# Three products of split operands in a pooling mixer, and attention's weight splits on VectorE

## Chip, cores and metric

One core of one Trainium2 chip runs the whole kernel. The metric is the device time of one execution in microseconds (us), as the median of the runs shown.

## What is computed

A two-layer backbone on 512 latent and 256 context tokens of 1024 channels, in float32. Layer 0 mixes tokens by pooling, layer 1 by attention; each layer ends in a squared-ReLU MLP, and each sub-layer is modulated by a shift, a scale and a gate that come from a conditioning vector. Cut to the part that the change touches:

```python
sh1, sc1, g1, sh2, sc2, g2 = jnp.split(s_lat @ ada_w[i] + ada_b[i], 6, axis=-1)   # the same for the context
a = rms_norm(h, norm_g[i, 0]) * (1 + sc1) + sh1
# pool_mix: each of 4 channel groups has its window (2, 4, 8, 16) and its own 256x256 matrix w
s = (sum of a over the window) / count - a
y = jnp.einsum("blgc,gcd->blgd", s, w) * pool_scale
h = h + g1 * y
m = rms_norm(h, norm_g[i, 1]) * (1 + sc2) + sh2
h = h + g2 * (square(relu(m @ w1)) @ w2)
```

Layer 1 is grouped-query attention with 8 query and 4 key heads of 128 channels, then its own MLP and a last RMSNorm of the latent tokens.

## The kernel before

Activations lie with channels on the partitions: `h_lat` (8 tiles of 128x512) and `h_ctx` (8 tiles of 128x256). A product of two float32 operands is made in one of two ways. Most are split: each operand is a pair hi + lo of type F32R, and three products (hi·hi, hi·lo, lo·hi, the table `PASSES`) are summed in PSUM. `hilo` (L85 to L87) makes such a pair: ScalarE writes hi, then VectorE, or the engine handed in, writes lo = source - hi. `load_w` loads 128x1024 of weights into one of two `raw` buffers and splits it. The other way is a plain F32 matmul, which stands in the trace as two records per instruction.

**The scales, shifts and gates.** `ada_w` comes in 12 blocks per layer. `ada0_products(b)` multiplies a block's four tiles with the conditioning vectors (L187) and copies the result to a row (L190, ScalarE); `ada0_done(b, row)` turns the row by four transposes (L196), and VectorE reduces it (L199), adds the bias (L201) and makes of it the scales `am` (L155, blocks 2, 3, 8, 9) or the gate `gp` (L163, blocks 4 and 5). Blocks 6 and 7 are the MLP's shift, blocks 8 and 9 its scale.

**The mixer of layer 0** runs so: the tokens are turned and normalized into `turned`; `pool_tile(k)` makes channel tile k of the pooled tokens with six plain F32 matmuls against banded matrices (L621) into a `mm` place of PSUM (two places of 4 KB), and ScalarE (odd k, L625) or VectorE (even k, L627) copies it to `pooled`. All eight tiles come first. The scale (1 + sc1) is not on the tokens but on the matrix: `scaled_weights` writes one copy of `pw` for the latent tokens (L634, ScalarE) and one for the context (L635, VectorE). Then `mix(dt)` makes output tile dt with four plain F32 matmuls (L645), `mixed(dt)` adds it to h under the gate (L348, VectorE), and `squares` gathers the squares for the next norm: ScalarE squares (L266), VectorE adds (L267). Blocks 4, 3, 5 and 6 stand between the eight tiles dt. After the loop come block 8's products, the sums of the squares (L282), the reciprocal root on GpSimd (L286), block 7's products, the spreading of the roots (L297), and then the MLP's first product, whose operand is made tile by tile: L705 and L727 on VectorE, L716 on ScalarE (for the context L703, L713, L714, L725), and used by L732.

**Attention** has for each key head two weight loads for the next queries (`q_fill`) and two for the output matrix (`wos`). Before, both of a `q_fill` and the second of each `wos` have their lo written by GpSimd, ten in all. Around them VectorE carries the softmax: maximum (L941), its negative bias (L943), the exponential on ScalarE (L946), the reciprocal (L948), the scaling (L949); and for the next queries the mean square (ScalarE L867, VectorE L868) and the rotation (L879 to L883). L961 are the transposes of the probabilities, L974 the values, L986 the output matrix, L860 the projections.

**What sets the order.** Every engine works through its queue in order. In the mixer TensorE's queue is the order in which the code is written; VectorE's and ScalarE's are set by the scheduler up to the line `stats = ps_aux()`, and from there to the MLP's first product by the code as well. All loads are on SyncE's queue, in the order of the code; a load waits there until its buffer is free, and all behind it wait too. `block6` and `block8` land in the places of `turned`, so they wait for the last pooled tile.

Of the kernel before, what the change touches and what calls it, by code (L numbers as in the profile page):

```python
# [14 lines left out]
P = 128  # L15
# [32 lines left out]
def dit_block_kernel(ctx: ExitStack, tc: tile.TileContext, xT, cols, adab, adaw, w1, w2, wqkv, wo,  # L48
# [119 lines left out]
    def ada0_products(b):  # L168

        ps = ps_aux()  # L170
        for u in range(4):
            if (b, u) in ((5, 3), (9, 3)):

                t = new(raws, [P, 1024], F32, "raw")
                nc.sync.dma_start(t, adaw[0, b, u])
            elif b in landing:
                t = landing[b][:, u]
                nc.sync.dma_start(t, adaw[0, b, u])
            elif early:
                t = early.pop(0)  # L180
            else:
                t = new(*praw)
                nc.sync.dma_start(t, adaw[0, b, u])
# [75 lines left out]
    def squares(acc, k, w, c0, n, place=None):  # L259
# [4 lines left out]
        else:  # L264
            sq = new(sc, [P, w, n], F32, "sc")
            act.activation(sq, hs(k, k + w, c0, n), AF.Square)  # L266
            dve.tensor_tensor(acc, acc, sq, op=ALU.add)  # L267
# [340 lines left out]
    pooled = [new(ap_, [P, 2, 2, T], F32, "act").rearrange("p a b n -> p (a b) n") for _ in range(2)]  # L608

    def pool_tile(k):  # L610

        g, ps = k // 2, ps_mm()
        w = WINDOWS[g] // 2
        for s, c0, n in segs:
            for i in range(n // P):
# [4 lines left out]
                o = c0 + i * P - PAD  # L620
                pe.matmul(ps[:, o + a : o + b], turned[s][:, i, k * P : k * P + P], bands[:, g, e, a:b],  # L621
                          start=i == 0, stop=i == n // P - 1, skip_group_check=True)
        dst = pooled[k // 4][:, k % 4]
        if k % 2:
            act.activation(dst, ps[:, :T], AF.Copy)  # L625
        else:
            dve.tensor_copy(dst, ps[:, :T])  # L627

    aw = [new(wp, [P, KT, 256], F32, "w") for _ in range(2)]

    def scaled_weights(k0, k1):

        for k in range(k0, k1):
            act.activation(aw[0][:, k], pw[:, k], AF.Copy, scale=am[0][0][:, k, 0:1])  # L634
            dve.tensor_scalar(aw[1][:, k], pw[:, k], am[0][0][:, k, 1:2], None, op0=ALU.mult)  # L635
# [3 lines left out]
    def mix(dt):  # L639

        ps = ps_mm()
        for s, c0, n in segs:
            for kc in range(2):
                k = dt // 2 * 2 + kc
                pe.matmul(ps[:, c0 : c0 + n], aw[s][:, k, dt % 2 * P : dt % 2 * P + P], pooled[k // 4][:, k % 4, c0 : c0 + n],  # L645
                          start=kc == 0, stop=kc == 1)
        return ps
# [3 lines left out]
    def mixed(dt, ps):  # L651
        for s, c0, n in segs:
            add_gated(dt, ps[:, c0 : c0 + n], gp, c0, n)
            if dt < KT - 1:
                accs[s] = squares(accs[s], dt, 1, c0, n)
            else:
                tails.append(new(sc, [P, 1, n], F32, "sc"))
                act.activation(tails[s], hs(dt, dt + 1, c0, n), AF.Square)

    row = ada0_products(2)  # L660
    pool_tile(0)
    ada0_done(2, row)
    scaled_weights(0, 4)
    for k in range(1, 8):
        pool_tile(k)

    for b, tag in ((6, "m_hi"), (8, "m_lo")):
        landing[b] = big.tile([P, 4, D], F32, tag=tag, name=f"block{b}")
    for dt in range(8):
        if dt % 2 == 0:  # L670
            b = (4, 3, 5, 6)[dt // 2]
            row = ada0_products(b)
        if dt == KT - 1:
            ws = [load_w(w1[0, t]) for t in range(2)]
        ps = mix(dt)
        if dt % 2 == 0:
            ada0_done(b, row)
            if b == 3:
                scaled_weights(4, 8)
        mixed(dt, ps)  # L680
    row = ada0_products(8)
# [5 lines left out]
    rrs = [rstd_cols(n, [accs[s], tails[s]], stats[:, 4 * s : 4 * s + n // P]) for s, _, n in segs]  # L687
    ada0_done(8, row)
    row = ada0_products(7)
    rbs = [spread(rrs[s], n, ps_aux()[:, :n]) for s, _, n in segs]  # L690
# [44 lines left out]
    for u in range(len(units) + 2):  # L735
# [7 lines left out]
        if u == 1:  # L743
            last = ada0_products(9)
            ada0_done(7, row)
# [292 lines left out]
    for n in range(8 * NKV):  # L1038
        g, half, i = n // 8, n // 4 % 2, n % 4
        if i == 0 and half == 0 and g + 1 < NKV:  # L1040
            fill = q_fill(g + 1, [load_w(wqkv[8 + 2 * (g + 1) + u], pool) for u in range(2)])
# [10 lines left out]
        if half == 0 and i == 1:  # L1052
            wos = [load_w(wo[2 * g + j], (dve, pool)[j]) for j in range(2)]
# [126 lines left out]
```

## Time and profile before

| | |
|---|---|
| median of 3 runs | 1269.24 us (1268.84 to 1270.68) |
| profiled execution, its own time | 1270.8 us |
| span of its trace | 1268.8 us |
| TensorE matmul busy | 97% |
| VectorE busy | 81% |
| ScalarE busy | 46% |
| GpSimd busy | 12% |

The profile is of one execution. Matmul (PE) and weight load (PEld) overlap; the ends of matmuls are modelled. Names such as `mm<-act,w` say what an instruction writes and reads; L followed by a number is a line of the kernel before. In the chain of waits each piece starts where the one ahead of it ended, so its length is what that work took of the path. In the change the lines from L621 on stand 6 to 18 lower in the file; texts here use the lines of before.

### The profile page before, as it was taken

The numbers are of one execution on the slowest core, as the hardware profiler recorded it, in microseconds if no ns is written. First come the engines' busy times: TensorE is split into PE (matmuls) and PEld (weight loads), VectorE is DVE, ScalarE is ACT, GpSimd is POOL, SyncE is SP. The second block draws the span as 40 slices with busy tenths as digits, with TensorE's granted clock in tenths as the row PEclk, the third lists the DMA queues.
The fourth block names the chain that finished last, engine by engine and source line by source line (L and its number), as shares of the span: only waits on it lengthen the run. The fifth ranks groups of instructions, "written<-read, shape, count | busy, mean of one in ns | idle before, by whom it ended". The sixth has DMA issues, their size and how long they took to land.

```text
span 1268.8 us, 20479 instructions
## 1 busy us (share of the span) xinstructions
PE 1236.7 (97%) x8150; PEld 1103.4 (87%) x8150; DVE 1026.2 (81%) x1752; ACT 588.7 (46%) x1052; POOL 149.1 (12%) x128
## 2 busy tenths in 40 slices
PE   7999999999999999999999999999999999999997
PEld 6567888899999999999888899899988898989896
DVE  6564999788989888866888378888899989898976
ACT  6455523443444444433465254445555444445443
POOL 0000000122121322231012121211000000000002
PEclk8999999999999999999999999999999999999998
DMA  9676414333433333311122011211223232323111
GB/s 352 259 275 219 147 67 153 113 117 117 149 114 133 121 127 120 121 67 34 45 81 85 23 61 34 67 34 67 84 67 116 100 133 71 130 76 125 67 34 67
DMA packets 41311, 138.67 MB, mean 109 GB/s; under 512 B 4736, under 2 KB 8064, under 8 KB 41088
## 3 DMA queue, kind: packets, MB, share of 16 engines
q1 hardware_dynamic: 41216, 137.36, 30.7%
q8 instruction: 64, 1.05, 0.3%
q14 instruction: 31, 0.25, 0.1%
HBM read 135.25 MB, written 2.10 MB: 108 GB/s over the span
## 4 chain that ended last, share of the span: by engine, by line
PE 62%; issue 27%; DVE 7%; ACT 2%; POOL 1%; DMA 1%; SPq 0%; POOLq 0%; DVEq 0%; ACTq 0%
PE mm L490 10%; PE aux L490 10%; PE aux L860 6%; PE mm L371 6%; PE aux L459 5%; PE mm L439 5%; PE aux L439 4%; PE aux L986 3%; PE aux L187 2%; PE mm L645 2%; PE mm L732 1%; PE aux L974 1%; PE aux L961 1%; PE mm L938 1%; PE mm L621 1%
## 5 line engine op out<-in xcount | busy, mean ns | idle before, releaser
L490 PE MATMUL mm<-act,w 128*128 128x512 f32 (+1 forms) x1224 | 237.7, 346 | 1.8 <-DVE h_lat L348 1.8
L490 PE MATMUL aux<-act,w 128*128 128x512 f32 (+1 forms) x1224 | 239.0, 346 | 0.2
L490 PEld LDWEIGHTS mm<-act,w 128*128 128x128 f32 x1224 | 195.1, 189 | 32.7 <-DVE h_lat L348 2.0
L490 PEld LDWEIGHTS aux<-act,w 128*128 128x128 f32 x1224 | 195.0, 189 | 29.5 <-DVE h_lat L348 0.6
L86 ACT ACTIVATE w<-raw 128x1024 fp32r<-128x1024 f32 x106 | 110.2, 1055 | 79.2 <-PE aux L490 37.8
L87 DVE TENSOR_TENSOR w<-raw,w 128x1024 fp32r<-128x1024 f32 x96 | 117.3, 1225 | 28.2 <-ACT w L86 27.5
L348 DVE SCALAR_TENSOR_TENSOR h_lat<-aux,mod,h_lat 128x512 f32<-128x512 f32 (+1 forms) x204 | 126.5, 629 | 16.0 <-PE aux L490 14.4
L428 POOL TENSOR_TENSOR sc<-pair 128x512 f32<-128x512 f32 x55 | 76.7, 1402 | 319.2 <-DVE h_lat L348 104.9
L348 DVE SCALAR_TENSOR_TENSOR h_lat<-mm,mod,h_lat 128x512 f32<-128x512 f32 (+1 forms) x140 | 97.7, 700 | 6.1 <-PE mm L490 3.7
L371 PE MATMUL mm<-m_m_hi,w 128*128 128x512 f32 (+1 forms) x320 | 92.4, 351 | 0.1
L860 PE MATMUL aux<-w,a_m_hi 128*128 128x256 f32 (+1 forms) x384 | 86.3, 320 | 0.0
L219 DVE SCALAR_TENSOR_TENSOR mc<-raw,s_f,mc 128x512 f32<-128x512 f32 x112 | 83.4, 763 | 2.0 <-DMA raw<-in_dram 1.3
L439 PE MATMUL mm<-m_m_hi,mc 128*128 128x256 f32 x384 | 71.0, 283 | 0.0
L286 POOL TENSOR_TENSOR sm<-sm,neghalf 128x2 f32<-128x2 f32 (+1 forms) x11 | 8.9, 811 | 509.9 <-DVE sm L284 509.9
L860 PEld LDWEIGHTS aux<-w,a_m_hi 128*128 128x128 f32 x384 | 63.4, 190 | 5.0
L459 PE MATMUL aux<-m_c,w 128*128 128x256 f32 x528 | 65.2, 283 | 0.0
L371 PEld LDWEIGHTS mm<-m_m_hi,w 128*128 128x128 f32 x320 | 56.1, 189 | 10.0 <-ACT r L379 0.8
L459 PEld LDWEIGHTS aux<-m_c,w 128*128 128x128 f32 x528 | 64.2, 192 | 0.0
L860 PE MATMUL aux<-w,a_m_lo 128*128 128x256 f32 (+1 forms) x192 | 61.2, 319 | 0.0
L439 PEld LDWEIGHTS mm<-m_m_hi,mc 128*128 128x128 f32 x384 | 60.7, 192 | 0.5
L371 PE MATMUL mm<-m_m_lo,w 128*128 128x512 f32 (+1 forms) x160 | 56.0, 351 | 0.0
L439 PE MATMUL mm<-m_m_lo,mc 128*128 128x256 f32 x192 | 54.4, 283 | 0.0
(244 smaller groups left out, 2509.1 us busy)
## 6 DMA issues: line engine op xcount, KB each, us to landing
raw<-in_dram SPq DMA_DIRECT2D x157, 512.0 KB, 3.3
praw<-in_dram SPq DMA_DIRECT2D x34, 512.0 KB, 8.1
fin<-in_dram SPq DMA_DIRECT2D x24, 512.0 KB, 4.2
pair<-in_dram SPq DMA_DIRECT2D x22, 512.0 KB, 4.6
block<-in_dram SPq DMA_DIRECT2D x8, 512.0 KB, 6.2
h_lat<-in_dram SPq DMA_DIRECT2D x4, 512.0 KB, 6.0
w<-in_dram SPq DMA_DIRECT2D x4, 512.0 KB, 10.7
out_dram<-fin SPq DMA_DIRECT2D x8, 256.0 KB, 2.6
```

The costliest lines, as they stand in the source:

```text
L86: act.activation(hi, src, AF.Copy)
L87: lo_eng.tensor_tensor(lo, src, hi.bitcast(F32), op=ALU.subtract)
L187: pe.matmul(ps[o : o + P // CG, :512], s_w[:, kt], t[:, kk * 512 : kk * 512 + 512], start=kt < CG, stop=kt >= KT - CG)
L219: dve.scalar_tensor_tensor(acc[:, s], w, scal, acc[:, s], op0=ALU.mult, op1=ALU.add)
L348: dve.scalar_tensor_tensor(h, ps, gate[:, dt, s : s + 1], h, op0=ALU.mult, op1=ALU.add)
L371: pe.matmul(ps[:, c0 : c0 + cn], lhs, ms(m, ax, k, c0, cn), start=k + wx + ax == 0, stop=k == KT - 1 and wx == 1)
L428: eng.tensor_tensor(t, x, y, op=how)
L439: pe.matmul(places[n], w[:, wx, k * P : k * P + P], inputs[n][ax][:, k], start=k + wx + ax == 0, stop=k == 3 and wx == 1)
L459: pe.matmul(pc[:, t * 256 : t * 256 + 256], ws[k // 4][:, wx, k % 4 * P : k % 4 * P + P], ms(m, ax, k, SEQ, CTX), start=k + wx + ax == 0, ...
L490: pe.matmul(ps, lhs, a[:, t, ax, c0 : c0 + n], start=t + wx + ax == 0, stop=t == 1 and wx == 1)
L860: pe.matmul(ps, lhs, ws[u][:, wx, o : o + width], start=k + ax + wx == 0, stop=k == KT - 1 and ax == 1)
L986: pe.matmul(ps[:, :256], ws[j][:, wx, dt * P : dt * P + P], o[:, ax, j], start=j + wx + ax == 0, stop=j == 1 and ax == 1)
```

## The change

1. The mixer's products are split. `scaled` takes a pooled tile out of PSUM, under the scale (1 + sc1) of its tokens, as a pair: ScalarE writes hi (512 and 256 columns apart), VectorE lo, by one instruction with the PSUM tile as its input. `pw` is split once, unscaled. `mix` has twelve F32R matmuls where it had four F32 ones.
2. The pooled tiles no longer come all first: four ahead of the loop, the others within it after dt = 1 to 4. Odd tiles use two of the four `aux` places instead of a `mm` place.
3. Blocks 2 and 4 are turned ahead of the loop (4 between tiles 1 and 3), blocks 3, 5 and 7 in it, block 6 at its end, block 8 behind the sums of squares; block 7 no longer stands between the roots and the MLP. Block 6's and 8's loads come behind block 9's first three on SyncE's queue.
4. In the loop GpSimd adds the squares (twelve adds), not VectorE.
5. The ten lo splits of attention's weights that GpSimd had go to VectorE.

```diff
@@ -171,7 +171,7 @@
         for u in range(4):
             if (b, u) in ((5, 3), (9, 3)):
-                t = new(raws, [P, 1024], F32, "raw")
+                t = new(mc, [P, 1024], F32, "mc")
                 nc.sync.dma_start(t, adaw[0, b, u])
             elif b in landing:
                 t = landing[b][:, u]
@@ -256,7 +256,7 @@
         k0, k = (k.start // 4, slice(k.start % 4, (k.stop - 1) % 4 + 1)) if isinstance(k, slice) else (k // 4, k % 4)
         return m[1][x][k0][:, k, c0 - SEQ : c0 - SEQ + n]
-    def squares(acc, k, w, c0, n, place=None):
+    def squares(acc, k, w, c0, n, place=None, eng=dve):
         if acc is None:
             acc = new(accp[0], [P, w, n], F32, accp[1]) if place is None else place
@@ -264,7 +264,7 @@
         else:
             sq = new(sc, [P, w, n], F32, "sc")
             act.activation(sq, hs(k, k + w, c0, n), AF.Square)
-            dve.tensor_tensor(acc, acc, sq, op=ALU.add)
+            eng.tensor_tensor(acc, acc, sq, op=ALU.add)
         return acc
     def all_squares(c0, n, place=None, k1=KT):
@@ -605,11 +605,17 @@
                 act.activation(t, t, AF.Copy, scale=rr[:, i : i + 1])
             else:
                 dve.tensor_scalar(t, t, rr[:, i : i + 1], None, op0=ALU.mult)
-    pooled = [new(ap_, [P, 2, 2, T], F32, "act").rearrange("p a b n -> p (a b) n") for _ in range(2)]
+    pooled = {}
     def pool_tile(k):
-        g, ps = k // 2, ps_mm()
+        g = k // 2
+        if k % 2:
+            places = [ps_aux(), ps_aux()[:, :CTX]]
+        else:
+            ps = ps_mm()
+            places = [ps[:, :SEQ], ps[:, SEQ:T]]
         w = WINDOWS[g] // 2
         for s, c0, n in segs:
             for i in range(n // P):
@@ -617,33 +623,35 @@
                 a = PAD if e == 1 else PAD + 1 - w
                 b = PAD + P if e == 2 else PAD + P + w
-                o = c0 + i * P - PAD
-                pe.matmul(ps[:, o + a : o + b], turned[s][:, i, k * P : k * P + P], bands[:, g, e, a:b],
+                o = i * P - PAD
+                pe.matmul(places[s][:, o + a : o + b], turned[s][:, i, k * P : k * P + P], bands[:, g, e, a:b],
                           start=i == 0, stop=i == n // P - 1, skip_group_check=True)
-        dst = pooled[k // 4][:, k % 4]
-        if k % 2:
-            act.activation(dst, ps[:, :T], AF.Copy)
-        else:
-            dve.tensor_copy(dst, ps[:, :T])
-    aw = [new(wp, [P, KT, 256], F32, "w") for _ in range(2)]
-    def scaled_weights(k0, k1):
-        for k in range(k0, k1):
-            act.activation(aw[0][:, k], pw[:, k], AF.Copy, scale=am[0][0][:, k, 0:1])
-            dve.tensor_scalar(aw[1][:, k], pw[:, k], am[0][0][:, k, 1:2], None, op0=ALU.mult)
+        return k, places
+    def scaled(k, places):
+        if k % 2 == 0:
+            pooled[k // 2] = new(ap_, [P, 2, 2, T], F32R, "act")
+        for s, c0, n in segs:
+            hi, lo = (pooled[k // 2][:, k % 2, x, c0 : c0 + n] for x in range(2))
+            a = am[0][0][:, k, s : s + 1]
+            act.activation(hi, places[s], AF.Copy, scale=a)
+            dve.scalar_tensor_tensor(lo, places[s], a, hi.bitcast(F32), op0=ALU.mult, op1=ALU.subtract)
+    aw = [new(wp, [P, KT, 256], F32R, "w") for _ in range(2)]
+    for k in range(0, KT, 4):
+        hilo(aw[0][:, k : k + 4], aw[1][:, k : k + 4], pw[:, k : k + 4])
     accs = [None, None]
     def mix(dt):
         ps = ps_mm()
-        for s, c0, n in segs:
-            for kc in range(2):
-                k = dt // 2 * 2 + kc
-                pe.matmul(ps[:, c0 : c0 + n], aw[s][:, k, dt % 2 * P : dt % 2 * P + P], pooled[k // 4][:, k % 4, c0 : c0 + n],
-                          start=kc == 0, stop=kc == 1)
+        for n, (kc, (wx, ax)) in enumerate((kc, p) for kc in range(2) for p in PASSES):
+            lhs = aw[wx][:, dt // 2 * 2 + kc, dt % 2 * P : dt % 2 * P + P]
+            for s, c0, w in segs:
+                pe.matmul(ps[:, c0 : c0 + w], lhs, pooled[dt // 2][:, kc, ax, c0 : c0 + w], start=n == 0, stop=n == 5)
         return ps
     tails = []
@@ -652,42 +660,52 @@
         for s, c0, n in segs:
             add_gated(dt, ps[:, c0 : c0 + n], gp, c0, n)
             if dt < KT - 1:
-                accs[s] = squares(accs[s], dt, 1, c0, n)
+                accs[s] = squares(accs[s], dt, 1, c0, n, eng=pool)
             else:
                 tails.append(new(sc, [P, 1, n], F32, "sc"))
                 act.activation(tails[s], hs(dt, dt + 1, c0, n), AF.Square)
     row = ada0_products(2)
-    pool_tile(0)
+    tile0 = pool_tile(0)
     ada0_done(2, row)
-    scaled_weights(0, 4)
-    for k in range(1, 8):
-        pool_tile(k)
-    for b, tag in ((6, "m_hi"), (8, "m_lo")):
-        landing[b] = big.tile([P, 4, D], F32, tag=tag, name=f"block{b}")
+    scaled(*tile0)
+    scaled(*pool_tile(1))
+    row = ada0_products(4)
+    scaled(*pool_tile(2))
+    ada0_done(4, row)
+    scaled(*pool_tile(3))
     for dt in range(8):
-        if dt % 2 == 0:
-            b = (4, 3, 5, 6)[dt // 2]
-            row = ada0_products(b)
-        if dt == KT - 1:
+        ps = mix(dt)
+        if dt in (0, 3):
+            row = ada0_products(3 + 2 * (dt > 0))
+        elif dt == 4:
+            ada0_done(5, row)
+        mixed(dt, ps)
+        if dt == 1:
+            ada0_done(3, row)
+        if dt in (1, 2, 3, 4):
+            scaled(*pool_tile(dt + 3))
+        if dt == 4:
+            for b, tag in ((6, "m_hi"), (8, "m_lo")):
+                landing[b] = big.tile([P, 4, D], F32, tag=tag, name=f"block{b}")
             ws = [load_w(w1[0, t]) for t in range(2)]
-        ps = mix(dt)
-        if dt % 2 == 0:
-            ada0_done(b, row)
-            if b == 3:
-                scaled_weights(4, 8)
-        mixed(dt, ps)
-    row = ada0_products(8)
+        if dt == 5:
+            row = ada0_products(7)
+        elif dt == 6:
+            ada0_done(7, row)
+    row = ada0_products(6)
     by_hand.enter_context(tc.manual_schedule(engines={mybir.EngineType.DVE, mybir.EngineType.Activation}))
     stats = ps_aux()
     rrs = [rstd_cols(n, [accs[s], tails[s]], stats[:, 4 * s : 4 * s + n // P]) for s, _, n in segs]
+    ada0_done(6, row)
+    row = ada0_products(8)
+    rbs = [spread(rrs[s], n, ps_aux()[:, :n]) for s, _, n in segs]
     ada0_done(8, row)
-    row = ada0_products(7)
-    rbs = [spread(rrs[s], n, ps_aux()[:, :n]) for s, _, n in segs]
     m = new_m("m")
     units = [u for k in range(0, KT, 2) for u in ((0, k, 1), (0, k + 1, 1), (1, k, 2))]
@@ -742,7 +760,6 @@
         if u == 1:
             last = ada0_products(9)
-            ada0_done(7, row)
         elif u == 3:
             ada0_done(9, last)
     ws = [load_w(w1[0, 2 + t]) for t in range(2)]
@@ -1038,7 +1055,7 @@
     for n in range(8 * NKV):
         g, half, i = n // 8, n // 4 % 2, n % 4
         if i == 0 and half == 0 and g + 1 < NKV:
-            fill = q_fill(g + 1, [load_w(wqkv[8 + 2 * (g + 1) + u], pool) for u in range(2)])
+            fill = q_fill(g + 1, [load_w(wqkv[8 + 2 * (g + 1) + u]) for u in range(2)])
         if 0 < n < 8 * NKV - 1:
             scores((n + 1) // 8, (n + 1) // 4 % 2, (n + 1) % 4, st)
         if i < 2 or g == NKV - 1:
@@ -1050,7 +1067,7 @@
         if i == 1 and n > 1:
             run(*prev)
         if half == 0 and i == 1:
-            wos = [load_w(wo[2 * g + j], (dve, pool)[j]) for j in range(2)]
+            wos = [load_w(wo[2 * g + j]) for j in range(2)]
         if pend:
             pend.pop()()
         turn(i, st)
```

**Where the order of the work changes.** ScalarE's queue at the first pooled tiles. `aux_328` (now `aux_330`) is block 2's product and `aux_422` (now `aux_374`) block 4's, each copied to its row by L190; L625 copies pooled tiles, L634 scales the matrix; in the change L638 is the hi of a pooled tile, and L86 here the hi of `pw`. Before:

```order
L190 ACTIVATE sc_337<-aux_328 128x512
L625 ACTIVATE act_324<-mm_364 128x768
L634 ACTIVATE w_326<-pw,am_137 128x256 x4
L625 ACTIVATE act_324<-mm_380 128x768
L625 ACTIVATE act_325<-mm_396 128x768
L625 ACTIVATE act_325<-mm_412 128x768
L190 ACTIVATE sc_431<-aux_422 128x512
```

Now:

```order
L190 ACTIVATE sc_339<-aux_330 128x512
L638 ACTIVATE act_357<-mm_341,am_137 128x512
L638 ACTIVATE act_357<-aux_362,am_137 128x512
L638 ACTIVATE act_357<-aux_363,am_137 128x256
L638 ACTIVATE act_357<-mm_341,am_137 128x256
L86 ACTIVATE w_324<-pw 128x1024 x2
L190 ACTIVATE sc_383<-aux_374 128x512
```

The four hi of tiles 0 and 1, which need block 2's scales, and the two hi of `pw` stand ahead of block 4's row, whose transposes TensorE now has two pooled tiles earlier than the loop.

VectorE's queue in attention, where the second head's queries have been projected and the weights for the third are split. Before (both splits are on GpSimd):

```order
L948 RECIPROCAL ri_7611<-rs_7609 128x1
L949 TENSOR_SCALAR r_7608<-r_7608,ri_7611 128x768
L868 TENSOR_SCALAR sm_7870<-sm_7870 128x4
L879 TENSOR_TENSOR sc_7881<-aux_7614,tabs 128x512
L87 TENSOR_TENSOR mc_7663<-aux_7664,mc_7663 128x256
```

Now (L965, L966, L885 and L896 are the lines L948, L949, L868 and L879 of before):

```order
L965 RECIPROCAL ri_7693<-rs_7691 128x1
L966 TENSOR_SCALAR r_7690<-r_7690,ri_7693 128x768
L87 TENSOR_TENSOR w_7809<-raw_7810,w_7809 128x1024
L87 TENSOR_TENSOR w_7814<-raw_7815,w_7814 128x1024
L885 TENSOR_SCALAR sm_7952<-sm_7952 128x4
L896 TENSOR_TENSOR sc_7963<-aux_7696,tabs 128x512
L87 TENSOR_TENSOR mc_7745<-aux_7746,mc_7745 128x256
```

Two splits now stand between a probability's scaling and the mean square of the next queries.

VectorE's queue where a head's output weights are split. Before (the second split is on GpSimd):

```order
L949 TENSOR_SCALAR r_8029<-r_8029,ri_8032 128x768
L87 TENSOR_TENSOR w_7895<-raw_7896,w_7895 128x1024
L943 TENSOR_TENSOR nb_8056<-mx_8054,sr_7878 128x1
L348 SCALAR_TENSOR_TENSOR h_lat<-aux_8072,mod_135,h_lat 128x256
L87 TENSOR_TENSOR mc_7983<-aux_8080,mc_7983 128x256
```

Now (L966 and L960 are L949 and L943 of before):

```order
L966 TENSOR_SCALAR r_8111<-r_8111,ri_8114 128x768
L87 TENSOR_TENSOR w_7977<-raw_7978,w_7977 128x1024
L87 TENSOR_TENSOR w_7982<-raw_7983,w_7982 128x1024
L960 TENSOR_TENSOR nb_8138<-mx_8136,sr_7960 128x1
L348 SCALAR_TENSOR_TENSOR h_lat<-aux_8154,mod_135,h_lat 128x256
L87 TENSOR_TENSOR mc_8065<-aux_8162,mc_8065 128x256
```

The second split stands ahead of the softmax's bias.

## Rows read from the trace of the kernel before

**Rows 1.** The page's head: span; busy time of TensorE and the other engines, instructions.

```profile
span 1268.8 us, 20479 instructions
PE 1236.7 (97%) x8150; PEld 1103.4 (87%) x8150; DVE 1026.2 (81%) x1752; ACT 588.7 (46%) x1052; POOL 149.1 (12%) x128
```

**Rows 2.** Chain of waits, first 140 us: start, length, what, records merged.

```profile
26.47 9.56 PE mm L621 x84
36.02 1.85 PE aux L187 x16
37.88 2.78 PE mm L645 x8
...
41.09 2.58 PE mm L645 x8
...
131.21 4.23 PE aux L490 x24
```

**Rows 3.** Busy time in the stretch of the mixing loop, 36.0 to 66.6 us.

```profile
36.00:66.60 30.60, 30.60 (x149) 15.07 (x151) 18.86 (x43) 13.12 (x25) 0.00 (x0) 1.00 0.68 260
```

**Rows 4.** Groups by form, 19 to 72 us: count, busy us, mean ns, idle before.

```profile
L348 DVE SCALAR_TENSOR_TENSOR h_lat<-mm,gp,h_lat 128x512 f32<-128x512 f32 x8 | 6.0, 749 | 3.7 <-PE mm L645 3.7
...
L348 DVE SCALAR_TENSOR_TENSOR h_ctx<-mm,gp,h_ctx 128x256 f32<-128x256 f32 x8 | 3.8, 475 | 0.0
...
L190 ACT ACTIVATE sc<-aux 128x512 f32<-128x512 f32 x6 | 3.5, 590 | 2.0 <-PE aux L187 2.0
L634 ACT ACTIVATE w<-pw,am 128x256 f32<-128x256 f32 x8 | 3.4, 497 | 0.5 <-DVE am L155 0.5
```

**Rows 5.** The page's DMA issues: MB landing in `block`, median us to landing.

```profile
block<-in_dram SPq DMA_DIRECT2D x8, 512.0 KB, 6.2
```

**Rows 6.** What TensorE's matmuls waited for, 19 to 130 us: us, times, longest.

```profile
PE mm L732 <- DVE m_m_lo L727: 1.6, 1, 1.6
PE mm L732 <- DVE m_c L725: 0.8, 1, 0.8
```

**Rows 7.** What TensorE's matmuls waited for, 690 to 910 us.

```profile
PE aux L961 <- DVE mc L87: 3.3, 2, 1.7
PE aux L986 <- DVE h_lat L348: 2.3, 2, 1.2
...
PE aux L986 <- DVE act L87: 0.7, 2, 0.4
```

**Rows 8.** VectorE in order of time, two stretches of attention: start, length, idle before.

```profile
761.80 2.35 DVE L868 TENSOR_SCALAR sm<-sm 128x4 f32<-128x4 f32 x1 [3.33 <-ACT sc L867]
...
785.94 0.17 DVE L868 TENSOR_SCALAR sm<-sm 128x4 f32<-128x4 f32 x1 [3.28 <-ACT sc L867]
...
790.10 0.15 DVE L943 TENSOR_TENSOR nb<-mx,sr 128x1 f32<-128x1 f32 x1
...
792.73 1.23 DVE L87 TENSOR_TENSOR w<-raw,w 128x1024 fp32r<-128x1024 f32 x1 [0.17 <-ACT w L86]
793.87 2.34 DVE L943 TENSOR_TENSOR nb<-mx,sr 128x1 f32<-128x1 f32 x1
```

**Rows 9.** GpSimd in order of time in the same stretches, 690 to 910 us.

```profile
759.39 4.73 POOL L87 TENSOR_TENSOR w<-raw,w 128x1024 fp32r<-128x1024 f32 x2 [18.00 <-ACT w L86]
...
793.73 2.47 POOL L87 TENSOR_TENSOR w<-raw,w 128x1024 fp32r<-128x1024 f32 x1 [5.90 <-ACT w L86]
```

**Rows 10.** ScalarE in order of time at two of attention's weight splits.

```profile
733.70 1.06 ACT L86 ACTIVATE w<-raw 128x1024 fp32r<-128x1024 f32 x1 [0.85 <-DMA raw<-in_dram]
...
758.25 1.06 ACT L86 ACTIVATE w<-raw 128x1024 fp32r<-128x1024 f32 x1 [0.62 <-issue]
759.68 1.06 ACT L86 ACTIVATE w<-raw 128x1024 fp32r<-128x1024 f32 x1 [0.38 <-PE aux L860]
```

**Rows 11.** GpSimd's costliest group, and the scales by VectorE over the whole run (min/median/max ns).

```profile
L428 POOL TENSOR_TENSOR sc<-pair 128x512 f32<-128x512 f32 x55 | 76.7, 1402 | 319.2 <-DVE h_lat L348 104.9 <-DVE op L434 88.8 <-DVE act L467 68.0
L155 DVE SCALAR_TENSOR_TENSOR am<-mod,pcol x8: 153/163/1258, 27.4 to 488.4; 128x8 f32<-128x8 f32 x6, 128x4 f32<-128x4 f32 x2
```

## Prediction

> **What bounds the kernel now.** I read the page's head first: TensorE has a matmul running for 1236.7 of 1268.8 us [rows 1], so time is won by giving it less to do, or by filling the few gaps that it has. Then the chain of waits at the start: from 26 to 66 us it is TensorE's own work in order, pooled tiles, then mixer products in pieces of 2.78 and 2.58 us [rows 2]; in that stretch TensorE is busy 30.60 of 30.60 us and VectorE 18.86 [rows 3]. Then TensorE's waits: two behind this loop, 1.6 and 0.8 us, both for VectorE's lo of the MLP's operand [rows 6], and in attention 6.3 us in three rows, all behind VectorE [rows 7]. For those I looked at VectorE in order of time. At 761.80 a mean square on four columns takes 2.35 us that takes 0.17 at 785.94, at 793.87 a softmax bias takes 2.34 us that took 0.15 at 790.10 [rows 8]; each time GpSimd had just begun a weight split, of 2.4 us each [rows 9]. So VectorE is held by GpSimd until the split is over, and TensorE runs dry behind it.
>
> **The mixer's products.** One `mix` is now a piece of 2.78 or 2.58 us, 2.68 in the mean [rows 2]. It becomes six pairs of a 512 and a 256 wide F32R matmul. The same pairs stand in the MLP's second product: 24 matmuls, 12 pairs, in 4.23 us [rows 2], so six pairs take 2.12 us. The loss is 0.56 us for each of eight tiles, all of it on TensorE's path: **-4.5 us**. The 0.35 us of a pair may be off by a few per cent; that is 0.3 us in all.
>
> **Evictions and splits around them.** VectorE's lo of a pooled tile is one instruction with its input in PSUM; the nearest rows are the gate's, 749 and 475 ns [rows 4], so 1.22 us for each of eight tiles, 9.8 us. It loses four copies, eight scalings and the twelve adds, together about as much, and gains two splits of `pw` at 1.23 [rows 8]. VectorE has 11.7 us free in the loop's 30.6 [rows 3], and a pooled tile (84 records, seven tiles of 12, take 9.56 us, so 1.37 each [rows 2]) is always at least a `mix` ahead of its use, so I cost these at nothing. If that cover went, each tile's eviction (ScalarE about 1.1, VectorE 1.22) would stand on the path at four places: up to 9 us, a rival below. The twelve adds on GpSimd come out at 1.40 us for 512 columns [rows 11] and, by half, about 0.7 for 256, 12.6 us in a loop of some 30; the last must be done by the sums of squares, 3.9 us of TensorE (one `mix` and block 6's products) behind the eighth gate's start: covered.
>
> **A row that comes too late.** Block 4's transposes now stand 4.6 us of TensorE's work behind block 2's (two pooled tiles at 1.37 and a block's products at 1.85 [rows 2]). ScalarE has ahead of block 4's row, from the moment that block 2's scales are there (three short steps on VectorE, the last of 0.16 us [rows 11], some 0.7 us with the handing over): two hi of 512 and two of 256 columns, by the rows 0.59 and 0.50 each [rows 4], and two hi of `pw` at 1.06 [rows 10], 4.3 us, then the row's own 0.59. With the 0.7 that is 5.6 against 4.6: I take **+0.9 us**, with 0 and 1.5 as ends.
>
> **Behind the loop.** Block 7's turn is out of VectorE's way, and block 8's comes in its place ahead of the operand's first tile. Block 9's products (1.85 us) now run between block 8's transposes and the first use, while VectorE and ScalarE make hi and lo in three steps of about 0.75 and three short ones. That leaves a wait of about 1.3 us where 1.6 was and about 0.6 where 0.8 was: **-0.5 us**, ends 0 and -2.4. Block 6's load waits for the last pooled tile; then TensorE has three `mix`, block 7's products and a turn, 3 x 2.12 + 1.85 = 8.2 us without the turn, and a block lands 6.2 us after issue [rows 5], so nothing is due here, and block 8, one block later in the same queue, has as much again. That sums to -4.1 us for layer 0's mixer.
>
> **Attention.** At two places like 761.80 both splits go into VectorE's queue ahead of the mean square. VectorE stood idle for 3.33 us there [rows 8], and ScalarE's two hi end at 759.31 and 760.74 [rows 10], so two splits of 1.23 end by 762.0 and the mean square comes at 762.0 instead of 764.0. The wait of 1.7 us that is TensorE's longest at L961 [rows 7] goes: 2 x 1.65 = **-3.3 us**. At two places like 793.87 a second split of 1.23 replaces 2.19 us of being held: 1 us each, and as the two gaps there add up to 3.0 us [rows 7] I take **-2.2 us**, ends 0 and -3.0. At the first head's output weights, the split waits in VectorE's queue for its hi at 734.76 [rows 10], and at the last head's there was no hold to win back: 1.23 us more in the queue at each, ends 0 and 2.5, I take **+1.3 us**, since VectorE has little idle time there. Attention: -4.2 us.
>
> **The sum**: -4.1 - 4.2 = -8.3 us against the profiled execution's 1270.8, so 1262.5; the median of the runs lies 1.6 us below that execution, so **1261.0 us**. At the good ends (-4.5 - 2.4, -6.3) it is 1256.0; at the bad ones (-4.5 + 1.5, -3.3 + 2.5) 1265.4.
>
> **A rule that speaks against it.** What the rows show: GpSimd holds VectorE while it reads SBUF [rows 8, 9], and a scale of 163 ns in the median once took 1258, beside GpSimd at work [rows 11]. The Trainium skill, page "SBUF — State Buffer", section "Who interferes with whom", says that a VectorE instruction with two SBUF inputs is blocked for the whole of a GpSimd instruction that reads SBUF, and one with its second input in PSUM is not. By that rule the lo of a pooled tile and the gate, with their input in PSUM, go free, as in the sum; but GpSimd, taken out of VectorE's way in attention, is put there in the loop, and the first rival has what that could cost. The trace agrees on L943, two of whose inputs lie in SBUF: 2.34 us for 0.15 [rows 8].
>
> **Rivals.**
>
> 1. *GpSimd's adds hold VectorE in the loop.* Seven of VectorE's instructions in the loop take all they read from SBUF: two weight splits, three bias adds, a scale, a gate. Held for 1.40 us each [rows 11] they lose 9.8 us. For it: the holds in attention. Against it: GpSimd is busy under half of the loop, and VectorE has 11.7 us free. All of it on the path would give 1261.0 + 9.8 = 1270.8. 5%.
> 2. *Attention gives nothing*: ten splits of 1.23 (12.3 us) take the place of about 11 us of holds (four of 2.2, two of some 1.2). For it: the total on VectorE hardly moves. Against it: the splits fall where VectorE is idle. 1261.0 + 4.2 = 1265.2. 17%.
> 3. *The loop's gain is lost to waits* between a pooled tile, its two evictions and the `mix` that needs the place; half of the 9 us above would do. Against it: no row of before shows such a wait. 1261.0 + 4.1 = 1265.1. 10%.
> 4. *Slower: the splits stop VectorE's queue.* A split waits for its hi, the hi for its load; GpSimd used to do that waiting, now the softmax stands behind it. If each of the ten costs its 1.23 and a wait of 0.85, as ScalarE's for the load at 733.70 [rows 10], that is 20.8 us, less the 6.3 of gaps and the 4.1: 1269.2 + 10.4 = 1279.6. It decides from seven of the ten on (7 x 2.08 exceeds 6.3 + 4.1 + 2.5). Against it: at 758.25 ScalarE is ahead of VectorE by over a microsecond. 6%.
> 5. *The change does less than it says*, both parts lost in part: about 1268. 4%.
>
> My forecast has the other 58%.
>
> **How the numbers follow.** A measurement of this kernel can tell about 0.2%, 2.5 us, from no change. The forecast's own range is 1256.0 to 1265.4; rivals 2 and 3 lie just inside its upper end. From 1256.5 to 1266.5 the forecast and these two are held but for some 5%, and rivals 1, 4 and 5 are left out: 80%. Faster (below 1266.7): 56 of the forecast, 24 of rivals 2 and 3: 0.80. Within: rivals 1 and 5 and 4 more: 0.13. Slower: 0.07.
>
> **What would show it.** A `mix` of 12 records in 2.1 us; a wait of about 0.9 us at block 4's transposes; no wait over 0.5 us between tiles of the loop; the MLP's first product some 4 us earlier; in attention no L943 or L868 over 0.3 us, and TensorE's waits there down from 6.3 us to 2 or 3. I am wrong if the loop's matmuls wait for evictions, if bias adds in the loop take over a microsecond and TensorE waits behind them, or if TensorE's waits in attention stay at 6 us with weight splits ahead of them.

## The result, and the profile after

The changed kernel takes 1263.61 us (median of 5 runs, 1262.69 to 1264.30), beside 1270.68 us for the kernel before on the same chip (5 runs, 1268.84 to 1271.71): a ratio of 0.9944, with a 95% interval of 0.9932 to 0.9957. That is 7.1 us less, where 8.3 had been forecast; 1261.0 was predicted with a range of 1256.5 to 1266.5, from a median before of 1269.24 in three runs. The profiled execution took 1262.69 us.

The head of its page, to be held beside [rows 1]:

```profile
span 1260.7 us, 20578 instructions
...
PE 1233.3 (98%) x8182; PEld 1105.2 (88%) x8182; DVE 1026.6 (81%) x1756; ACT 591.9 (47%) x1058; POOL 137.2 (11%) x130
```

The span is 8.1 us shorter, but TensorE is busy for only 3.4 us less: more than half of the gain is idle time of TensorE. VectorE's total has not moved, as the rows of the change would have it (it gave up work in the mixer and took ten splits).

**Where the 8.1 us came from** is read by taking the same matmul in both traces and comparing its start:

| the same matmul | before, us | after, us | earlier by |
|---|---|---|---|
| first sum of squares behind the mixer | 68.48 | 65.06 | 3.42 |
| first product of layer 0's MLP with a lo (called the MLP's first product below) | 79.81 | 77.78 | 2.03 |
| a product of layer 0's MLP, past all its ada blocks | 389.67 | 387.85 | 1.82 |
| last head of attention, output product | 893.17 | 885.88 | 7.30 |
| first product of layer 1's MLP behind attention's norm | 916.05 | 907.94 | 8.12 |

So the mixer's loop gave 3.4 us and 1.6 of them were lost behind it, attention gave 5.5, and 0.8 came at its end. Each piece has its lines.

The mixer, in the chain of waits of the kernel after (start, duration, what):

```profile
26.97 1.99 ACT act L638 x4
28.97 1.89 ACT w L86 x2
30.86 0.50 ACT sc L190
31.35 0.04 issue
31.40 0.66 PE aux L196 x4
32.05 1.34 PE aux L627 x12
33.40 2.11 PE mm L654 x12
...
40.12 1.36 PE mm L627 x12
41.48 2.08 PE mm L654 x12
...
63.20 1.85 PE aux L187 x16
...
68.30 0.87 PE aux L196 x4
69.17 3.12 PE aux L187 x16
72.28 1.53 PE aux L297 x12
```

A `mix` (L654) is 2.08 to 2.12 us, or 2.32 in the two behind a block's products, where it was 2.58, or 2.78 behind a block's products [rows 2]. The stretch without a wait runs from 36 to 65 us: every piece starts where the one ahead of it ends. The last lines are the surprise. Four transposes (L196) take 0.87 us that take 0.44 elsewhere, and block 8's products (L187) 3.12 where block 6's, at 63.20, take 1.85: 1.7 us more for the same work. The stretches of the same profile say why (stretch, its length, busy time of PE, PEld, DVE, ACT and POOL, then granted clock, DMA share and GB/s):

```profile
36.00:65.06 29.06, 29.06 (x209) 21.13 (x200) 16.75 (x34) 15.28 (x29) 12.44 (x12) 1.00 0.76 296
65.06:68.00 2.94, 2.59 (x23) 2.54 (x23) 0.16 (x1) 0.60 (x1) 0.79 (x1) 1.00 1.04 419
68.00:72.00 4.00, 4.00 (x23) 1.36 (x22) 0.52 (x3) 0.00 (x0) 0.93 (x2) 0.57 1.03 410
72.00:78.00 6.00, 4.83 (x38) 2.62 (x35) 3.43 (x8) 2.75 (x5) 0.00 (x0) 1.00 0.75 291
```

For most of 68 to 72 us the granted clock was at the lower of its two levels (1.2 GHz). What TensorE did just before are the sums of squares, matmuls of 128x1, where the weight loads (PEld) are busy for 2.54 of 2.94 us.

Attention's waits of TensorE in the kernel after, against [rows 7]:

```profile
PE aux L943 <- DVE sc L900: 1.8, 2, 0.9
PE mm L297 <- POOL sm L286: 0.8, 1, 0.8
PE aux L919 <- DVE sc L915: 0.5, 1, 0.5
PE aux L297 <- POOL sm L286: 0.4, 1, 0.4
PE aux L978 <- DVE r L966: 0.4, 1, 0.4
```

The 6.3 us of three rows behind VectorE's splits and residual adds are gone; new is one of 0.9 at two places, for the next query's rotation (L900). VectorE in order of time, at the place that answers to 761.80 in [rows 8]:

```profile
756.99 1.23 DVE L87 TENSOR_TENSOR w<-raw,w 128x1024 fp32r<-128x1024 f32 x1 [1.05 <-ACT w L86]
758.43 1.23 DVE L87 TENSOR_TENSOR w<-raw,w 128x1024 fp32r<-128x1024 f32 x1 [0.22 <-ACT w L86]
759.58 0.16 DVE L885 TENSOR_SCALAR sm<-sm 128x4 f32<-128x4 f32 x1
```

The two splits fall into VectorE's idle time, behind their hi, and the mean square takes 0.16 us instead of 2.35 and is over at 759.7 instead of 764.2; 2.3 us of that come from ahead of this place, the rest is won here. No mean square and no softmax bias of attention takes over 0.18 us now.

The last 0.8 us are no work of the change. The stretch at the end of attention in the kernel before:

```profile
902.00:906.00 4.00, 3.87 (x20) 3.88 (x21) 2.82 (x7) 2.78 (x6) 0.07 (x1) 0.58 0.00 0
```

It ran at a granted clock of 0.58, and the same stretch after ran at 1.00. The two profiles thus had their drops at different places: after lost 1.7 us at 68, before 0.8 at 902.

### The profile page after: what moved, and what is told of

It reads as the page before. It is cut to its first block, busy times and chain, and to the rows that moved or that the text cites. A ratio compares the mean times of both kernels' runs of the same rounds, so it can differ in the third digit from the quotient of the medians.

```text
span 1260.7 us, 20578 instructions
## 1 busy us (share of the span) xinstructions
PE 1233.3 (98%) x8182; PEld 1105.2 (88%) x8182; DVE 1026.6 (81%) x1756; ACT 591.9 (47%) x1058; POOL 137.2 (11%) x130
## 4 chain that ended last, share of the span: by engine, by line
PE 65%; issue 27%; DVE 5%; ACT 1%; POOL 1%; DMA 1%; SPq 0%; POOLq 0%; DVEq 0%; ACTq 0%
PE mm L490 10%; PE aux L490 10%; PE aux L877 8%; PE mm L371 6%; PE aux L459 5%; PE mm L439 5%; PE aux L439 4%; PE aux L1003 3%; PE aux L991 2%; PE aux L187 2%; PE mm L955 1%; PE aux L978 1%; PE mm L654 1%; PE mm L750 1%; DVE h_lat L348 1%
## 5 line engine op out<-in xcount | busy, mean ns | idle before, releaser
L87 DVE TENSOR_TENSOR w<-raw,w 128x1024 fp32r<-128x1024 f32 x106 | 129.4, 1225 | 31.8 <-ACT w L86 31.5
L86 ACT ACTIVATE w<-raw 128x1024 fp32r<-128x1024 f32 x106 | 110.2, 1055 | 78.7 <-PE aux L490 38.1
L348 DVE SCALAR_TENSOR_TENSOR h_lat<-aux,mod,h_lat 128x512 f32<-128x512 f32 (+1 forms) x204 | 126.6, 630 | 16.3 <-PE aux L490 14.7
L348 DVE SCALAR_TENSOR_TENSOR h_lat<-mm,mod,h_lat 128x512 f32<-128x512 f32 (+1 forms) x140 | 97.9, 701 | 6.1 <-PE mm L490 4.2
L219 DVE SCALAR_TENSOR_TENSOR mc<-raw,s_f,mc 128x512 f32<-128x512 f32 x112 | 84.0, 768 | 1.4 <-DMA raw<-in_dram 0.6
```

The costliest lines, as they stand in the source:

```text
L86: act.activation(hi, src, AF.Copy)
L87: lo_eng.tensor_tensor(lo, src, hi.bitcast(F32), op=ALU.subtract)
L219: dve.scalar_tensor_tensor(acc[:, s], w, scal, acc[:, s], op0=ALU.mult, op1=ALU.add)
L348: dve.scalar_tensor_tensor(h, ps, gate[:, dt, s : s + 1], h, op0=ALU.mult, op1=ALU.add)
```

## The experiments

All ratios are to the kernel before on the chip of the same group of runs (a, b or c); its medians there were 1271.15, 1271.47 and 1272.19 us. A ratio is not quite that of the two medians.

| run | what it is | median, us | ratio, 95% interval |
|---|---|---|---|
| a1 | mixer part alone | 1269.67 | 0.9985 (0.9974 to 0.9995) |
| a2 | attention part alone | 1266.46 | 0.9961 (0.9949 to 0.9973) |
| a4 | mixer, query weights | 1264.58 | 0.9948 (0.9931 to 0.9964) |
| a5 | mixer, output weights | 1270.62 | 0.9991 (0.9981 to 1.0002) |
| b0 | the change again | 1263.09 | 0.9939 (0.9926 to 0.9953) |
| b1 | + wide sums | 1261.69 | 0.9922 (0.9909 to 0.9935) |
| b2 | + query turned early | 1261.19 | 0.9919 (0.9906 to 0.9932) |
| b3 | adds on VectorE | 1263.39 | 0.9942 (0.9926 to 0.9958) |
| c1 | + wide sums, query early | 1261.00 | 0.9910 (0.9896 to 0.9925) |
| c2 | c1, all sums wide | 1260.22 | 0.9904 (0.9891 to 0.9916) |
| c3 | c2, second layer's blocks later | 1259.82 | 0.9904 (0.9891 to 0.9916) |
| c4 | before + wide sums | 1271.25 | 0.9993 (0.9985 to 1.0002) |

**a1 and a2: each part alone.** In a1 attention's ten splits go back to GpSimd; a2 is the kernel before with that edit the other way.

```diff
-            fill = q_fill(g + 1, [load_w(wqkv[8 + 2 * (g + 1) + u]) for u in range(2)])
+            fill = q_fill(g + 1, [load_w(wqkv[8 + 2 * (g + 1) + u], pool) for u in range(2)])
-            wos = [load_w(wo[2 * g + j]) for j in range(2)]
+            wos = [load_w(wo[2 * g + j], (dve, pool)[j]) for j in range(2)]
```

a1: 

> The changed kernel with attention's weight splits given back to GpSimd as before (both of the next head's query weights, the second of each head's output weights); everything in the mixer stays changed. Theory (GpSimd's splits of 2.4 us held VectorE, and TensorE ran dry behind it: between the two traces attention's own part is 5.5 us): 1263.6 + 5.5 = 1269.1 us, and the profile shows again two mean squares and two softmax biases of 2.3 us each, and TensorE's waits in attention at 6 us or more. Rival (attention gives nothing, the mixer gave all): 1263.6. Second question, on the 1.7 us that went in layer 0 beside a granted clock of 0.57 between 68 and 72 us: the mixer is the same here, so if the products around the sums of squares always bring it, the drop is there again at the same place; if it comes by the chance of an execution, it may be gone and the first MLP product starts 1.7 us earlier.

a2: 

> The kernel before with attention's weight splits alone moved to VectorE; the mixer is as before. Theory: 1270.7 - 5.5 = 1265.2 us. Rival 2 of the prediction (attention gives nothing): 1270.7. If the first and the last head cost what the prediction put there (1.3 us), 1270.7 - 4.2 = 1266.5.

a1 came to 1269.67, as the theory has it, and TensorE's waits of [rows 7] are back to the tenth:

```profile
PE aux L978 <- DVE mc L87: 3.3, 2, 1.7
PE aux L1003 <- DVE h_lat L348: 2.3, 2, 1.2
PE aux L1003 <- DVE act L87: 0.7, 2, 0.4
PE aux L978 <- DVE r L966: 0.3, 1, 0.3
```

a2 came to 1266.46, 4.7 us under before (by the interval 3.4 to 6.5). The drops of the clock put aside, the traces give attention 5.2 us in a2 against before, and 5.7 in the change against a1. The mixer alone (a1 against before) is worth 1.9 us by the ratio (0.6 to 3.3), 1.5 by the medians. Rival 2 (attention gives nothing) falls. The clock: a1's profile has the drop (the stretch at the lower level) at the same place, 69.0 us. So has a2's, with the mixer of before, a little later, where the profile of before has none. The stretch in a2:

```profile
72.00:76.00 4.00, 4.00 (x21) 1.50 (x19) 0.53 (x3) 0.60 (x1) 0.42 (x1) 0.57 0.38 135
```

and in before, the stretch that answers to it:

```profile
71.00:75.00 4.00, 4.00 (x35) 2.40 (x36) 0.69 (x4) 0.60 (x1) 1.43 (x2) 1.00 0.39 129
```

With a drop at that place in both, like for like, the first product of the MLP is at 81.23 in a2 and at 77.78 after the change: the mixer's gain is then 3.45 us and not 2.0.

**a4 and a5: which splits.** One of the two lines of the diff above each.

a4: 

> The changed kernel, with the second output weight of each head split by GpSimd again and the query weights left on VectorE. Theory: the mean squares stay at 0.17 us and the softmax biases go back to 2.34 at two places, worth 2.2 us by the prediction: 1263.6 + 2.2 = 1265.8. Rival (the two places aren't independent: the gain needs both, or either gives all of it): 1269.1 or 1263.6.

a5: 

> The changed kernel, with the next head's query weights split by GpSimd again and the output weights left on VectorE. Theory: the mean squares go back to 2.35 us at two places, worth 3.3 us: 1263.6 + 3.3 = 1266.9. Rival (not independent): 1269.1 or 1263.6. By the theory this run and the one with the query weights alone lose together what the run with both given back loses.

The gains are not independent: a4 came to 1264.58, 1.2 us under its theory, and a5 to 1270.62, 3.7 over it. Against a1, the query weights alone shorten attention by 4.7 us (drops put aside), the output weights alone make it 0.45 longer; on top of the query weights the output weights give 1.0. TensorE's waits in attention in a5 show why:

```profile
PE aux L978 <- DVE mc L87: 3.3, 2, 1.7
PE aux L943 <- DVE sc L900: 1.8, 2, 0.9
PE aux L978 <- DVE sc L898: 1.2, 1, 1.2
PE aux L978 <- DVE r L966: 0.4, 1, 0.4
```

The output splits take the waits for L348 away, but while GpSimd still holds VectorE at the queries, a wait of 1.2 us behind the rotation (L898) comes in the first head. (This profile is of the longest of a5's runs, and the granted clock in it reads 0.95 instead of 1.00 throughout; between the places where the waits differ, the same matmuls stand as far apart as in a1.)

**b0: the change again.**

> The changed kernel once more, as it is, beside the kernel before. In its first profile the granted clock was 0.57 between 68 and 72 us, behind the sums of squares, and 1.7 us of layer 0's gain went there. Theory (the place brings it, in both kernels, but not in every execution): the drop is there again or it is not, and where it is not, the first MLP product starts at about 76.1 us instead of 77.8; the median stays at 1263 to 1264.5. Rival (the change alone brings it, always): it is there, with 1.7 us, and no execution comes under 1262.

The median is 1263.09. The drop is there again, at 69.8 us, which theory and rival both allow; the rival wanted no run under 1262, and the fastest took 1261.85, too near to decide. What speaks against the rival is a2: its mixer is the old one, and its profile has the drop. Single runs go from 1261.85 to 1267.72, and the profile, which is of the longest one, shows what a long one has more: the lower clock at four places, about 70, 131, 636 and 899 us. By the same matmuls in the first profile of the change and in this one, 2.5 of the 5.0 us between them are lost from 105 to 140 us, 1.5 at 636 and 0.8 at 899. In the first of these stretches it also has a wait that the first profile had not:

```profile
PE aux L777 <- DVE s_w L772: 1.7, 1, 1.7
```

VectorE there, in order of time:

```profile
124.08 0.16 DVE L201 TENSOR_TENSOR mod<-sm,bcol 128x8 f32<-128x8 f32 x1
126.91 0.75 DVE L219 SCALAR_TENSOR_TENSOR mc<-raw,s_f,mc 128x512 f32<-128x512 f32 x1 [2.67 <-DMA raw<-in_dram]
127.58 0.18 DVE L199 TENSOR_REDUCE sm<-aux 128x8 f32<-128x32 f32 x1
```

VectorE's queue stands 2.67 us before a multiply with a row of the second layer's blocks that has not landed (L219), and behind it stand the reduce and the bias (L199, L201) on which the rest of the mixer's shift waits. This wait is 1.1 to 1.7 us in a1, a4, b0 and b3, 0.3 in c2, and in none of the three profiles with the old mixer.

**b1 and c4: the sums of squares 64 columns wide.** The extra columns hold the same sums and are not read.

```diff
-    rrs = [rstd_cols(n, [accs[s], tails[s]], stats[:, 4 * s : 4 * s + n // P]) for s, _, n in segs]
+    rrs = [rstd_cols(n, [accs[s], tails[s]], stats[:, 256 * s : 256 * s + n // P * 64], 64) for s, _, n in segs]
...
-                pe.matmul(ps[:, i : i + 1], x[:, i * P : i * P + P], ones[:, :1], start=j == 0, stop=j == len(sums) - 1)
+                pe.matmul(ps[:, i * cols : i * cols + cols], x[:, i * P : i * P + P], ones[:, :cols], start=j == 0, stop=j == len(sums) - 1)
```

b1: 

> The changed kernel, with the 24 matmuls of the sums of squares behind the mixer 64 columns wide instead of one (the other 63 columns hold the same sums again and are not read). Theory on the clock (what lies ahead of the drop are 128x1 products, whose weight loads alone take the time): the drop at 68 to 72 us is gone, the sums take no more than 0.3 us longer, the first MLP product starts at 76.1 to 76.4 us, and the time falls by about 1.3 to 1.7 against executions that have the drop: 1262. Rival 1: the drop stays, 1263.6 to 1264. Rival 2: the wide matmuls take more time than the drop did, 1265.

c4: 

> The kernel before, with only the sums of squares behind the mixer 64 columns wide. It asks whether the drop of the clock behind these sums is there before the change as well (it was absent in the profile of before and present, with 1.5 us, in the profile of before with attention's splits moved). If before has it as often as the changed kernel: 1.4 us less than before. If the change alone brings it: the same as before within 0.5 us.

b1, the stretch that answers to 68 to 72 us above:

```profile
68.00:72.00 4.00, 4.00 (x36) 2.40 (x35) 0.52 (x3) 0.60 (x1) 0.92 (x2) 1.00 1.03 410
```

The clock stays at its upper level (2.4 GHz), 36 matmuls pass in 4 us where 23 did, the sums themselves take 0.1 us longer, and the first product of the MLP starts at 76.14 us, 1.64 earlier. With narrow sums the changed mixer has the drop in all 7 profiles taken, with wide ones (b1, c1, c2, c3) in none of 4. The median falls by 1.4 us; the intervals of the two ratios overlap, so the time of the step rests on the trace. All of it can't be counted as won: b1's profile has a drop at 632 us, where the first profile of the change has none, and loses 1.5 us there. In c4, on the old mixer, wide sums gave 0.9 us, between -0.3 and +1.9: neither answer is excluded. But c4 can be compared with b1, c1 and c2 free of this drop: the MLP's first product is at 80.10 us in c4 and at 76.14, 76.36 and 76.27 in the three, so the mixer's own gain is 3.7 to 4.0 us there. Whether the change makes this drop more frequent, or before had it as often, is left open (of two profiles of the old mixer with narrow sums one has it).

**b2: the query rotated earlier.**

```diff
+        if i == 0 and n > 0:
+            step(prev)
         if i == 1 and n > 1:
             run(*prev)
```

> The changed kernel, with the rotation of the next query one step earlier (at the first quarter of each half head instead of the second), ahead of the residual adds of the output. Theory (the two waits of 0.91 us that are left in attention are for that rotation, behind four residual adds on VectorE): they go, 1263.6 - 1.8 = 1261.8 us. Rival (VectorE's order there is set by the work in all and not by where the step stands): no change, 1263.6; a loss up to 2 us if the softmax comes later for it.

The waits of 0.91 us are gone; TensorE's waits in the heads are now these two:

```profile
PE aux L991 <- ACT act L86: 0.3, 1, 0.3
PE aux L978 <- DVE r L966: 0.2, 1, 0.2
```

Attention is 1.2 us shorter than in b0 by the traces, less than the 1.8 expected, and the median 1.9 us lower.

**b3: the adds on VectorE again.**

```diff
-                accs[s] = squares(accs[s], dt, 1, c0, n, eng=pool)
+                accs[s] = squares(accs[s], dt, 1, c0, n)
```

> The changed kernel, with the twelve adds of squares on VectorE again instead of GpSimd. Rival 1 of the prediction (GpSimd's adds hold VectorE in the loop): faster, by up to the 9.8 us put there. Theory (no hold shows in the trace, and VectorE is idle for a third of the loop): the same within 0.5 us, or slower by up to 1 us where an add stands ahead of the eviction that the next tile waits for.

1263.39 us, the same as b0, where rival 1 of the prediction had up to 9.8 us: it falls. On VectorE the adds bring one wait of 0.2 us into the loop, on GpSimd none. Rival 1's hold was not put to the test, though: in the profile after, none of the seven instructions that it names was on VectorE during an add of GpSimd but for a scale and a weight split, which had begun first. The evictions and gates that did run beside an add (at 42.28 and 56.51 us, say) took their usual 0.75 us.

**c1, c2, c3: the edits together.** c2 makes 64 columns the default of `rstd_cols`; c3 starts `ada1_block` at chunk 3 instead of 2.

c1: 

> The changed kernel with both edits that helped: the sums of squares behind the mixer 64 columns wide, and the next query's rotation one step earlier. Theory (two separate causes, a clock drop in layer 0 and a wait in attention): 1263.1 - 1.4 - 1.9 = 1259.8 us, no granted clock under 1.00 between 66 and 80 us, and no wait of 0.91 us in attention. Rival (the drop only moves to the next place where TensorE has little to do): 1261.2.

c2: 

> As the run with both edits, and every other sum of squares (the norms behind the first and the last layer's MLP and behind attention) 64 columns wide too. Theory: a drop that stood at about 900 us in some profiles, with 0.8 us, comes less often: 0 to 0.8 us less than with both edits. Rival (the wide sums wait for nothing else and cost their own time): up to 0.5 us more.

c3: 

> As the run with all sums wide, and the blocks of the second layer's shift and scale, which VectorE multiplies from loaded rows, begin one chunk of the MLP later. Theory (what took 0.5 to 1.7 us at 125 to 130 us in four profiles is VectorE's queue standing before such a row that has not landed, with the last blocks of the mixer's shift behind it): the wait at about 127 us is gone in every execution, 0.5 to 1 us less than with all sums wide. Rival (the rows are late at the new place too): the same.

All three are faster than the change, by about 0.3%: ratios of 0.9910 and 0.9904 where the change again had 0.9939. That the two edits add up (1259.8) is not shown: c1's 1261.0 lies at its rival's 1261.2, and its interval overlaps those of b1 and b2. No drop stands between 66 and 80 us in any of them, and no wait of 0.9 us in attention. A drop at 630 to 632 us is there in all three, and c1 has one at 895 as well; with all sums wide (c2, c3) there is none at 895, but two profiles are few. Of the changed kernels with narrow sums three of seven profiles have a drop at 630 to 638 us, of those with wide sums four of four: that the drop in part moves there, as c1's rival says, is not excluded. c3 has no wait at 127 us; its time equals c2's, whose profile has 0.3 us there, so what the move is worth is below what these runs can tell. c2 is the version to keep: it beats both kernels (before by 12 us, the change by some 4) with two small edits.

## Why the prediction was right

The total held, in part by luck: layer 0 gave 1.8 us in the profile instead of 4.1, attention 5.5 instead of 4.2, and 0.8 came from a drop of the clock that the profile of before happened to have. The mechanisms were right but for one, the clock.

- **The mixer's products, -4.5.** Right: eight pieces of 2.08 to 2.32 us, 2.12 forecast; they add up to 17.2 us where the old ones made 21.4, so -4.2.
- **Evictions, splits and adds at nothing.** Right: TensorE has no wait between 36 and 65 us. GpSimd's adds took 12.4 us (12.6 estimated), and VectorE's instructions that read SBUF alone (L201 and its like) stay at 0.16 to 0.17 us; no add of GpSimd was running when one of them began (b3). Only the reverse hold shows: one add took 1.81 us instead of 1.29, begun at 45.59 while a split on VectorE ran from 45.03 to 46.24. The Trainium skill, page "SBUF — State Buffer", section "Who interferes with whom", says that the one that issues first has the shared ports and the other blocks; the trace agrees on both sides, in attention before and here.
- **A row that comes too late, +0.9.** The place and the cause were right, the size was not: the wait at block 4's transposes is 0.23 us after, 0.3 to 0.4 in most of the other profiles. ScalarE's queue is the one forecast, each piece a little shorter (four hi of 1.99 us in all, two of `pw` of 1.89, then the row), and TensorE's two pooled tiles and the products ahead of the transposes took 5.1 us instead of 4.6. That longer work is on the path as well, so the place cost about 0.7 us after all.
- **Behind the loop, -0.5.** At the operand's first tile two waits of 0.5 and 0.7 us stand in place of one of 1.6, and that of 0.8 is gone; of this 0.24 us came through at the MLP's first product, with drops like for like (a2 against after) and with none (c4 against b1). Then the step failed that the sum never had: it took the clock at its upper level throughout, and the drop behind the sums of squares took 1.7 us in that profile. With it layer 0 gave 1.8 us in the trace and 1.9 (0.6 to 3.3) in a1, instead of 4.1; without the drop (c4 against b1, c1 and c2) it is 3.7 to 4.0 at the MLP's first product. A wait of VectorE for a row that had not landed takes up to 1.7 us more in some executions.
- **Attention, -4.2.** Right in its mechanism, too small: 5.2 to 5.7 us by the traces, 4.7 (3.4 to 6.5) in a2. The query weights were put at 3.3 and gave 4.7: the two places gave 2.0 and 2.1 us (a4 against a1) instead of 1.65, because the sum counted the one long wait of each place alone, and the first head gave 0.6 more, where 0.3 of wait stood. The output weights were put at -2.2 + 1.3 = -0.9 and gave -1.0 on top of the query weights, and this is luck: by place (the change against a4) the two middle heads gave 0.6 us each, 1.2 and not 2.2, since waits of 0.9 each for the next rotation (L900) came in place of the 3.0 us of waits for L348 and L87, and the first and the last head together lost 0.3 and not 1.3. That the output weights gain nothing by themselves (a5) was not foreseen.
- **The rivals.** 1 fell by b3 and 2 by a2. Of 3 and 4 the profile after has no sign: no `mix` waits for an eviction (in b3 one does, for 0.2 us), and the splits fall into VectorE's idle time. What 5 said, that the change does less than it says, is true of the mixer alone, for a cause that 5 did not name.

## What to carry to other kernels

A weight split on GpSimd is not free when VectorE has instructions such as the softmax's bias or the mean square coming: count the hold, and see whether VectorE's own idle time has room for the work. When work is taken off TensorE's path, read the granted clock of the stretch behind it too, in more than one execution: here matmuls of one column kept the engine's row full and still stood ahead of a drop, and 64 columns cost 0.1 us for 24 of them. And give back one half of a change at a time: here one half alone gained nothing, and on top of the other half it gained 1.0 us.

## What the runs showed of the hardware that was not expected

The drops of TensorE's clock come at few places, and by execution. Over the 14 profiles they began, the ramp at the start and the end apart, only at 67 to 73 us (behind the sums of squares), at 131 to 133 (behind two waits in a row, of 1.5 or 1.7 and of 0.5 us), at 630 to 638 (behind a wait of 1.8) and at 894 to 905 (behind a wait of 0.8 and the next norm's sums); each costs some 0.8 to 1.7 us, and about 3 where the first lasted twice as long (a5 and b3). The profile after had one of the four, that of b0 all four; with the wait at 127 us, which also comes by execution, the three that after lacks make 4.8 of the 5.0 us between these two profiles. That the other runs of one kernel differ for the same reason is likely, and not shown. The Trainium skill, page "TensorE: Matmul & The Clock Gate", section "Part 1: The HAM clock gate", ties the lower level to an idle engine; the traces agree in part at 630 to 638 us, where the wait of 1.8 us stands in all 14 profiles and the drop in eight of them, but at 68 us the engine's row was busy for 2.59 of 2.94 us, and matmuls of 64 columns in place of one kept the upper level (b1).
